# Storing the last staged batch of a sliding-window copy in parts, the rows that may spill first

## The chip, the cores and the metric

The kernel runs on one core of a Trainium2 chip. The metric is the device time of one execution in microseconds (us), lower is better. The program does no arithmetic at all: it only moves data with the core's 16 DMA engines.

## The reference

The input is a float32 array of 32 batches, 4096 rows of 256 values. The output holds 127 windows per batch, each of 64 rows, one starting every 32 rows.

```python
def setup_inputs():
    batch, length, dim = (32, 4096, 256)
    window_size = 64
    stride = 32
    ...

def reference(x, window_size, stride):
    batch, length, dim = x.shape
    n_windows = (length - window_size) // stride + 1
    result = np.zeros((batch, n_windows, window_size, dim), dtype=np.float32)
    for i in range(n_windows):
        start = i * stride
        result[:, i] = x[:, start:start + window_size].copy()
    return result
```

Call 32 rows (32 KB) a block. A batch has 128 blocks, and window w is block w followed by block w + 1. So almost every block is written twice, as half 0 of one window and as half 1 of the one before it.

## The kernel before

Three queues work at once.

- The Sync queue copies windows of the "direct" batches from DRAM to DRAM.
- The Scalar queue serves eleven "staged" batches (1, 4, ... 31). It loads a batch into on-chip memory, one block per partition, and stores it twice, once as all the halves 0 and once as all the halves 1. A store has 128 partitions but a batch has only 127 windows, so a store writes a row or two past its own batch. These spilled rows land in a neighbouring batch's windows, which must be written afterwards.
- The GpSimd queue writes those neighbours' windows, each after the staged stores beside it have landed.

The last staged batch is 31. Its stores spill into windows 125 and 126 of batch 30, and the Sync queue repairs these with one 128 KB copy at the very end.

```python
    def store(self, q, t, b, half, shift):
        w = b * self.nw - half - shift
        return q.dma_start(
            out=self.oap(2 * w + half, [[2 * self.blk, self.nb], [1, self.blk]]),
            in_=t[:, :],
            max_dma_last_dim=OUT,
        )
...
    # class Staging
    def store(self, q, g):
        n, i = divmod(g, len(self.tiles))
        q.wait_ge(self.loaded[i], 16 * (n + 1))
        for half in (0, 1):
            self.c.store(q, self.tiles[i], self.batches[g], half, self.shift(g)).then_inc(self.stored[i], 16)
...
        # GpSimd queue
        count(c.windows(ring_r, last, 112, 4), rest)
        count(c.columns(ring_r, last, 116, 9), rest)
        # Sync queue: the last copy, windows 125 and 126 of batch 30
        st.wait_stored(ring_d, len(staged) - 1)
        count(c.columns(ring_d, last, 125, 2), done)
        for sem in (done, near, rest):
            ring_d.wait_ge(sem, total[sem])
```

Of the kernel before, what the change touches and what calls it, by code (L numbers as in the profile page):

```python
# [11 lines left out]
class Copier:  # L12
# [36 lines left out]
    def load(self, q, t, b, shift):  # L49

        return q.dma_start(
            out=t[:, :],
            in_=self.xap(b * self.nb - shift, [[self.blk, self.nb], [1, self.blk]]),
            max_dma_last_dim=IN,
        )

    def store(self, q, t, b, half, shift):


        w = b * self.nw - half - shift  # L60
        return q.dma_start(
            out=self.oap(2 * w + half, [[2 * self.blk, self.nb], [1, self.blk]]),
            in_=t[:, :],
            max_dma_last_dim=OUT,
        )


class Staging:


    def __init__(self, c, tc, pool, dtype, batches, bufs, shifts):
# [2 lines left out]
        self.loaded = [tc.alloc_semaphore(f"loaded{i}") for i in range(bufs)]  # L74
        self.stored = [tc.alloc_semaphore(f"stored{i}") for i in range(bufs)]

    def shift(self, g):
        return self.shifts.get(self.batches[g], 0)

# [6 lines left out]
    def store(self, q, g):  # L86
        n, i = divmod(g, len(self.tiles))
        q.wait_ge(self.loaded[i], 16 * (n + 1))
        for half in (0, 1):
            self.c.store(q, self.tiles[i], self.batches[g], half, self.shift(g)).then_inc(self.stored[i], 16)  # L90

    def wait_stored(self, q, g):
        n, i = divmod(g, len(self.tiles))
# [12 lines left out]
@with_exitstack  # L106
def kernel(
    ctx: ExitStack,
    tc: tile.TileContext,
    x: bass.AP,  # L110
    window_size: bass.AP,
    stride: bass.AP,
    out: bass.AP,
):
    nc = tc.nc
    W, S = int(window_size), int(stride)
    B, L, D = x.shape
    n_win = (L - W) // S + 1
    assert out.shape == (B, n_win, W, D)
    c = Copier(x, out, B, L, D, W, S, n_win)  # L120
    staged = [*range(1, B, 3)]
    direct = [b for b in range(B) if b not in staged]
    pool = ctx.enter_context(tc.tile_pool(name="xb", bufs=1))



    st = Staging(c, tc, pool, x.dtype, staged, 6, {0: -1, B - 1: 1})
    ring_d, ring_s, ring_r = nc.sync, nc.scalar, nc.gpsimd
    done = tc.alloc_semaphore("done")
    near = tc.alloc_semaphore("near")  # L130
    rest = tc.alloc_semaphore("rest")
    total = {done: 0, near: 0, rest: 0}

    def count(dma, sem):
        dma.then_inc(sem, 16)
        total[sem] += 16

    per, loads, stores = 6, 6 * 17, 34
    todo = 7 * len(direct)
    turns = share = 0  # L140
    with tc.tile_critical():  # L141
        st.run(ring_s)

        for b in direct:
            w = 0 if b - 1 not in staged else 8 if b + 1 in staged and b + 1 < B - 1 else 15
            for j in range(7):
                todo -= 1
                sem = near if todo == 2 else done
                share += 90 if turns % (loads + per * stores) < loads else 12
                if share >= 120:  # L150
                    share -= 120
                    turns += 4
                    count(c.windows(ring_d, b, w, 16, 0), done)
                    count(c.windows(ring_d, b, w, 16, 1), sem)
                else:
                    turns += 3
                    count(c.windows(ring_d, b, w, 16), sem)
                w += 16
                if todo == 7:
                    count(c.windows(ring_d, B - 1, c.nw - 1, 1, 1, 2048), done)  # L160
                    if 0 in staged:
                        count(c.windows(ring_d, 0, 0, 1, 0, 2048), done)

        ring_r.wait_ge(near, 16)
        pieces = (32768,)
        last = B - 2
        for i, b in enumerate(direct[:-1]):
            for g, n in enumerate(staged):
                if abs(n - b) == 1:
                    st.wait_stored(ring_r, g)  # L170
            parts = [(0, 15)] if b - 1 in staged else [(112, 15)]
            if b - 1 in staged and b + 1 in staged:
                parts = [(0, 8), (120, 7)]
            for w, n in parts:
                count(c.windows(ring_r, b, w, n, None, pieces[i % len(pieces)]), rest)


        count(c.windows(ring_r, last, 112, 4), rest)
        count(c.columns(ring_r, last, 116, 9), rest)
        st.wait_stored(ring_d, len(staged) - 1)  # L180
        count(c.columns(ring_d, last, 125, 2), done)
        for sem in (done, near, rest):
            ring_d.wait_ge(sem, total[sem])


# [33 lines left out]
```

## Time and profile before

| | |
|---|---|
| time, three runs | 752.45 us median (752.31 to 753.29) |
| time, five runs | 753.07 us median (752.31 to 753.29) |
| span of the execution in the trace | 743.6 us |
| summed rate over the span | 421 GB/s |

The trace is of an execution that was about 1% quicker than the timed ones.

From the page of the kernel before. The rows are the busy share of the DMA engines and their rate in 40 slices of the span; then the packets; then each queue's packets, MB and share of the 16 engines' time (q1 is the Sync queue, q10 the Scalar queue, q0 the GpSimd queue); then what was read from and written to DRAM.

```profile
span 743.6 us, 309 instructions
DMA  9999999999999999999999999999999999999995
GB/s 369 430 429 433 433 437 428 425 422 434 422 420 419 438 423 414 431 428 423 423 431 413 424 427 436 432 426 428 433 425 433 423 427 432 423 426 436 423 428 241
DMA packets 18098, 313.26 MB, mean 421 GB/s; under 512 B 4144, under 2 KB 4144, under 8 KB 4336
q1 hardware_dynamic: 7952, 154.32, 48.9%
q10 hardware_dynamic: 8976, 138.41, 43.9%
q0 software_dynamic: 1168, 20.51, 6.5%
HBM read 220.95 MB, written 267.09 MB: 656 GB/s over the span
```

The engines never rest until the last slice. The "under 512 B" packets are completion packets of 4 bytes: in this trace the Sync queue's 200 DMAs have 3200 of them and the Scalar queue's 33 have 528, 16 to a DMA, as many as there are engines, and just as many increments of their semaphores are recorded. They took 9 ns in the mean.

The waits of the Sync queue (us in total, times, longest), and the issue of its last copy in the timeline (start, duration), both of the kernel before:

```profile
SPq L44 <- DMA out_dram<-xb: 179.3, 1, 179.3
SPq L141 <- DMA out_dram<-in_x_dram: 1.2, 1, 1.2
SPq L183 <- DMA out_dram<-in_x_dram: 0.6, 1, 0.6
```

```profile
738.18 0.58 SPq L44 DMA_DIRECT2D out_dram<-in_x_dram  x1
```

L44 is the copy: it waits for the stores until 738.18. Then the GpSimd queue's last landing is waited for (L183, 0.6 us, until 739.40), and then the copy's own landing (L141, 1.2 us more). This 1.2 us is what the change can hide.

### The profile page before, as it was taken

The page shows a single profiled execution, that of the slowest core. Times are in us where ns is not written, and L with a number is a line of the kernel's source. Part 1 is how long each engine was busy: PE and PEld are TensorE (multiplying, and loading weights), DVE is VectorE, ACT ScalarE, POOL GpSimd, SP SyncE. Part 2 cuts the span into 40 slices and gives each one's busy share as a digit, 9 for nine tenths or more (in the row PEclk, how much of TensorE's full clock was granted, in tenths as well). Part 3 has the DMA queues.
Part 4 walks back from the last instruction along what each step waited for, and adds up shares of the span by engine and source line. Part 5 has one row for each costly group of instructions (what it writes and reads, how often), then busy time and mean ns, then how long its engine had stood idle before and what let it go on. Part 6 is the DMA issues. An engine that isn't in the chain of part 4 may idle for free.

```text
span 743.6 us, 309 instructions
## 1 busy us (share of the span) xinstructions
POOL 12.8 (2%) x26
## 2 busy tenths in 40 slices
POOL 0000000000000000000000000000000000130100
DMA  9999999999999999999999999999999999999995
GB/s 369 430 429 433 433 437 428 425 422 434 422 420 419 438 423 414 431 428 423 423 431 413 424 427 436 432 426 428 433 425 433 423 427 432 423 426 436 423 428 241
DMA packets 18098, 313.26 MB, mean 421 GB/s; under 512 B 4144, under 2 KB 4144, under 8 KB 4336
## 3 DMA queue, kind: packets, MB, share of 16 engines
q1 hardware_dynamic: 7952, 154.32, 48.9%
q10 hardware_dynamic: 8976, 138.41, 43.9%
q0 software_dynamic: 1168, 20.51, 6.5%
q14 instruction: 2, 0.02, 0.0%
HBM read 220.95 MB, written 267.09 MB: 656 GB/s over the span
## 4 chain that ended last, share of the span: by engine, by line
another core or an unknown queue 92%; POOL 2%; issue 0%; POOLq 0%; SPq 0%
POOL out_dram L34 2%; POOL out_dram L44 0%; POOLq L214 0%; SPq L141 0%; POOLq L94 0%
## 5 line engine op out<-in xcount | busy, mean ns | idle before, releaser
L34 POOL DMA_DIRECT2D out_dram<-in_x_dram x21 | 12.0, 576 | 686.7 <-DMA out_dram<-in_x_dram 647.0
L44 POOL DMA_DIRECT2D out_dram<-in_x_dram x1 | 0.6, 581 | 0.0
L200 POOL MEMSET const-float32-0.0<- 128x1 f32 x1 | 0.1, 99 | 0.2 <-issue 0.2
L200 POOL MEMSET const-bfloat16-1.0<- 128x1 bf16 x1 | 0.1, 102 | 0.0
L200 POOL MEMSET const-float32-1.0<- 128x1 f32 x1 | 0.1, 99 | 0.0
L200 POOL MEMSET const-uint8-127<- 128x1 uint8 x1 | 0.1, 99 | 0.0
## 6 DMA issues: line engine op xcount, KB each, us to landing
out_dram<-in_x_dram SPq DMA_DIRECT2D x96, 1024.0 KB, 100.8
out_dram<-xb ACTq DMA_DIRECT2D x22, 4096.0 KB, 142.5
out_dram<-in_x_dram SPq DMA_DIRECT2D x102, 512.0 KB, 89.1
xb<-in_x_dram ACTq DMA_DIRECT2D x11, 4096.0 KB, 122.0
out_dram<-in_x_dram POOLq DMA_DIRECT2D x20, 960.0 KB, 37.8
out_dram<-in_x_dram POOLq DMA_DIRECT2D x1, 576.0 KB, 40.3
out_dram<-in_x_dram POOLq DMA_DIRECT2D x1, 256.0 KB, 36.8
out_dram<-in_x_dram SPq DMA_DIRECT2D x1, 128.0 KB, 2.5
```

The lines of the kernel that those rows point to most:

```text
L34: return q.dma_start(out=self.oap((b * self.nw + w0) * 2 + h, [[2 * blk, n], row]), in_=self.xap(b * self.nb + w0 + h, [[blk, n], row]), m ...
L44: return q.dma_start(out=self.oap((b * self.nw + w0) * 2, [[part, 16], [2 * self.blk, n], row]), in_=self.xap(b * self.nb + w0, [[part, 16 ...
L200: nc = _bacc.Bacc("TRN2", target_bir_lowering=False, num_devices=1)
```

## The change

The intent is to issue the last copy before the stores are finished. The rows that may spill are partitions 0 and 1 of half 1 and partition 0 of half 0. So half 1 goes out first, then partitions 0 to 31 of half 0, and only these count for the copy's wait. The other 96 partitions follow on a semaphore of their own. That four of the parts take 16 partitions each, 4 apart, was my guess at a quicker shape; no record of the kernel before showed it.

```diff
-    def store(self, q, t, b, half, shift):
-        w = b * self.nw - half - shift
+    def store(self, q, t, b, half, shift, p0=0, n=128, step=1):
+        w = b * self.nw - half - shift + p0
         return q.dma_start(
-            out=self.oap(2 * w + half, [[2 * self.blk, self.nb], [1, self.blk]]),
-            in_=t[:, :],
+            out=self.oap(2 * w + half, [[2 * step * self.blk, n], [1, self.blk]]),
+            in_=t[p0 : p0 + (n - 1) * step + 1 : step, :],
             max_dma_last_dim=OUT,
         )
 ...
+        self.ended = tc.alloc_semaphore("ended")
 ...
-        for half in (0, 1):
-            self.c.store(q, self.tiles[i], self.batches[g], half, self.shift(g)).then_inc(self.stored[i], 16)
+        parts = [(0, 0, 128, 1), (1, 0, 128, 1)]
+        if g == len(self.batches) - 1:
+            parts = [(1, 0, 128, 1), (0, 0, 32, 1)]
+            rest = [(0, 96, 32, 1)] + [(0, 32 + k, 16, 4) for k in range(4)]
+        for half, *p in parts:
+            self.c.store(q, self.tiles[i], self.batches[g], half, self.shift(g), *p).then_inc(self.stored[i], 16)
+        if g == len(self.batches) - 1:
+            for half, *p in rest:
+                self.c.store(q, self.tiles[i], self.batches[g], half, self.shift(g), *p).then_inc(self.ended, 16)
+            self.ended_total = 16 * len(rest)
 ...
-        for sem in (done, near, rest):
-            ring_d.wait_ge(sem, total[sem])
+        total[st.ended] = st.ended_total
+        for sem, n in total.items():
+            ring_d.wait_ge(sem, n)
```

## The prediction

The sum of the prediction came to 752.45 - 0.95 + 0.35 = 751.85 us. The +0.35 us was my estimate, of 0.2 to 1 us, for longer packets of the partial stores, and what it rested on was not shown.

> **What bounds the kernel now.** It only moves data. The page's slice row shows the 16 DMA engines at 9 tenths in 39 of 40 slices, about 425 GB/s; the packet records give 27 GB/s per engine, one packet open on each (16 KB out of SBUF 0.61 us, 32 KB DRAM to DRAM 1.21 us). The change removes no bytes, so only the last slice (5 tenths, 241 GB/s) can gain.
>
> **The tail before**, from semaphore landings and packets, in us of the 743.6 us span:
> - One engine runs 2 us behind the other 15 (the second store of the last staged batch lands on 15 engines by 736.07, on the last at 738.16). The others have no data packets from 736.8; the late one works until 738.94.
> - The Sync queue waits for both whole stores of that batch, because a few rows spill into batch 30's windows 125 and 126. It issues the 128 KB copy of these windows at 738.18; first packets 739.55, landing 740.65.
> - The GpSimd queue's last copy lands at 739.38 on the late engine, whatever happens to the stores. The last wait ends at 740.67; some 3 us of closing barriers follow.
>
> So only 740.65 - 739.38 = 1.27 us of the copy is exposed.
>
> **What the change does.** The rows that can spill (half 1, then partitions 0 to 31 of half 0) are stored first and counted alone. Per engine 12 of 32 packets follow them, about three quarters of the 22.5 us of one whole store, so the copy should be issued at about 721 and land by 726, hidden. Its packets remain: two of 0.16 us per engine, 0.32 us, now before the end on the late engine. Gain: 1.27 - 0.32 = 0.95 us. Added: five DMAs on the Scalar queue (five 9 ns completion packets per engine; issue about 0.5 us each when unblocked, over 100 us ahead of need) and one wait of 0.03 us.
>
> [...] No record of this kernel shows a partial store. In the tail stores get about 188 GB/s (GpSimd's copies the other 240)[...].
>
> **Time.** 752.45 - 0.95 + 0.35 = 751.85; I say 751.8 us, range 750.9 to 752.8. Faster by over 2%: 0.01; within: 0.98; slower: 0.01.
>
> **What would show it.** Right: the copy is issued near 721; the final wait ends near 739.7 to 740.2, released by the late engine's GpSimd or store landing; the summed rate stays near 430 GB/s, with store packets over 0.61 us only between about 717 and 728. Wrong: the copy is still issued after 735, or its landing ends the span, or partial stores' packets take 1.2 us.
>
> **What would make it wrong.** [...] parts that use fewer than 16 engines; the late engine lagging more, or not at all (then the gain could reach 2 us); noise: the three runs before span 1 us, as much as the effect.

## The result

The changed kernel took 752.92 us (median of five, 751.71 to 753.81) against 753.07 us before (752.31 to 753.29). The ratio is 1.0001, 95% interval 0.9988 to 1.0015: the same time. In a second set of five, on another occasion, it was 1.0000 (0.9987 to 1.0012). A ratio is the mean time of one kernel's fast runs over that of the other's of the same rounds, so it is not quite the ratio of the medians. The prediction, 751.8 us with a range to 752.8, missed.

The same lines of the page of the changed kernel:

```profile
span 752.0 us, 315 instructions
GB/s 370 425 424 419 431 425 430 425 422 420 420 411 420 429 419 418 422 410 427 418 416 410 419 422 430 430 427 431 431 423 418 421 421 431 417 416 427 422 413 251
DMA packets 18178, 313.26 MB, mean 417 GB/s; under 512 B 4224, under 2 KB 4224, under 8 KB 4416
q10 hardware_dynamic: 9056, 138.41, 44.0%
HBM read 220.95 MB, written 267.09 MB: 649 GB/s over the span
```

Only q10 has more packets, 9056 - 8976 = 80. These are five more DMAs with 16 completion packets each. The waits of the Sync queue and the copy in the timeline, of the changed kernel:

```profile
SPq L44 <- DMA out_dram<-xb: 168.0, 1, 168.0
SPq L195 <- DMA out_dram<-in_x_dram: 15.5, 1, 15.5
```

```profile
732.53 0.58 SPq L44 DMA_DIRECT2D out_dram<-in_x_dram  x1
```

So the early copy works as meant. It is issued at 732.53 and has landed by 741.34, and the Sync queue then waits 15.5 us for the GpSimd queue's last copy. The wait for the copy's landing has gone from the end. Yet the time did not change.

**How the end was compared.** For each trace I took the moment at which 20 MB were still to be moved, and cut the time from there to the end of the span into four terms:

- *mean finish*: the mean time per engine that is filled with data packets (checked again from the packet records: their times after that moment, summed and divided by 16, agree within 0.1 us), leaving out the late copy where the copy comes after everything else. Small packets and gaps are not in it; they fall into the next term;
- *late engine*: how long after that the last engine finishes;
- *landing*: from the last of these data packets to the last landing of any DMA;
- *closing*: the barriers after the last landing.

| trace | mean finish | late engine | landing | closing | sum |
|---|---|---|---|---|---|
| before | 46.13 | 3.06 | 1.71 | 2.99 | 53.89 |
| before, r1 | 46.85 | 1.62 | 1.65 | 3.00 | 53.12 |
| before, r7 | 46.99 | 1.65 | 1.62 | 3.00 | 53.25 |
| change | 47.48 | 3.08 | 0.42 | 3.43 | 54.40 |
| change, r2 | 47.85 | 3.22 | 0.46 | 3.42 | 54.95 |
| change, r8 | 47.54 | 2.32 | 0.43 | 3.43 | 53.72 |

Landing fell by 1.22 us in the mean, close to the 1.27 us that the prediction read from the trace. Closing rose by 0.43 us and mean finish by 0.97 us (46.66 to 47.62), and these two took it back. The late engine scatters by 1.5 us between traces of one and the same kernel. The mean finish of before leans on its first trace, the quicker execution. Between traces of the same occasion mean finish rose by 1.00 us (r1 to r2) and by 0.55 us (r7 to r8).

### The profile page after: what moved, and what is told of

The parts are those of the page before. It is cut to its first block, busy times and chain, and to the rows that moved or that the text cites. A ratio compares the mean times of both kernels' runs of the same rounds, so it can differ in the third digit from the quotient of the medians.

```text
span 752.0 us, 315 instructions
## 1 busy us (share of the span) xinstructions
POOL 12.8 (2%) x26
## 3 DMA queue, kind: packets, MB, share of 16 engines
q1 hardware_dynamic: 7952, 154.32, 48.7%
q10 hardware_dynamic: 9056, 138.41, 44.0%
q0 software_dynamic: 1168, 20.51, 6.6%
HBM read 220.95 MB, written 267.09 MB: 649 GB/s over the span
## 4 chain that ended last, share of the span: by engine, by line
another core or an unknown queue 92%; POOL 2%; issue 0%; POOLq 0%; SPq 0%
POOL out_dram L34 2%; POOL out_dram L44 0%; POOLq L226 0%; SPq L152 0%; POOLq L105 0%
```

## The experiments

The expectations name these theories. Theory a: stores of parts with 32 partitions in a row are slow, which loses what the early copy gains, and parts with partition step 4 are not (the reason that I supposed is not shown by any run). Theory b: the gain is there and the scatter of the bulk hides it. Theory c: the order of the last waits costs 0.43 us. Theory d: the parts hurt by where their rows lie in DRAM. Theory e: parts cost nothing in the bulk. Theory f came last: every packet of a queue, however small, uses up the queue's turn on its engine. "Shape theories" are a and d, which blame the parts' partitions or rows.

### Replicas, and the two halves of the change (r1 to r4)

r1 is the kernel before and r2 the changed kernel, unaltered. r3 keeps the parts and gives up the early copy; r4 keeps the early copy and uses parts that all have partition step 4.

```diff
 r3, from the change
         st.wait_stored(ring_d, len(staged) - 1)
+        ring_d.wait_ge(st.ended, st.ended_total)
         count(c.columns(ring_d, last, 125, 2), done)
 r4, from the change
-            parts = [(1, 0, 128, 1), (0, 0, 32, 1)]
-            rest = [(0, 96, 32, 1)] + [(0, 32 + k, 16, 4) for k in range(4)]
+            parts = [(1, 0, 128, 1), (0, 0, 32, 4)]
+            rest = [(0, k, 32, 4) for k in range(1, 4)]
```

> The kernel before, run against itself, for the noise and for a second trace of its tail. Both theories [...] expect a ratio of 1.000 with an interval of about 0.15% either way. In its trace the copy of windows 125 and 126 should be issued within 1 us of the last landing of the stores and land 2.3 to 2.7 us later, the stores' packets of the last 40 us should take 0.61 to 0.62 us in the mean, and the data packets of 15 engines should end within 3 us of each other.

> The changed kernel again, for a second trace and ten timed runs in all. Theory a [...]: the stores' packets of the last 40 us again take about 3% over 0.611 us in the mean, the summed rate falls to about 400 GB/s between the first partial store and the four parts, and the engines' last data packets spread over about 5 us where before they spread over 2 us beside the late engine. Theory b (noise only): packets at 0.611 us, spread as before, and the last landing 1 us nearer to the end of the bulk. Ratio 0.999 to 1.001 in both.

> The stores in parts as in the change, but the Sync queue waits for all parts before it issues the copy, so the splitting is there and the early copy is not. Against the kernel before it shows the cost of the parts alone: theory a expects 1 to 2.5 us more (ratio 1.0015 to 1.003), theory b expects the same time (below 1.0005). In its trace the copy should be issued right after the last part lands and the span should end about 3 us plus 2.5 us after that.

> The early copy kept, but half 0 of the last batch goes out as four parts of 32 partitions with partition step 4 (0, 4, ... 124 first, it holds the spilling row)[...]. Theory a expects the tail's store packets back at 0.61 to 0.62 us, the copy still issued about 15 us before the end, and the gain of about 1 us to appear (ratio 0.998 to 1.000). Theory b expects what the changed kernel shows.

The kernel before ran at 755.33 us here.

| run | median us | ratio to before (95%) | mean finish | late engine | landing | closing | sum |
|---|---|---|---|---|---|---|---|
| r1, before | 755.18 | 0.9990 (0.9977 to 1.0003) | 46.85 | 1.62 | 1.65 | 3.00 | 53.12 |
| r2, change | 755.67 | 1.0000 (0.9987 to 1.0012) | 47.85 | 3.22 | 0.46 | 3.42 | 54.95 |
| r3, parts only | 755.70 | 1.0008 (0.9995 to 1.0021) | 47.10 | 2.41 | 2.56 | 2.99 | 55.05 |
| r4, step 4 | 754.72 | 0.9996 (0.9979 to 1.0013) | 47.43 | 2.49 | 0.42 | 3.42 | 53.77 |

The time alone cannot settle half a microsecond: the interval is about 1 us either way, and even before against itself comes out at 0.9990. The traces say more. (A figure "from 8 to 3 MB left" and the like is my own sum over the trace's packet records in the stretch in which that much was still to be moved.) The parts raise the mean finish even without the early copy (r3), and parts with step 4 raise it too (r4). Against theory a, the DRAM copies' packets in the tail were as much too long as the stores' (in r2 from 8 to 3 MB left, 4.7% over 1.213 us and 4.7% over 0.611 us; in r1 2.0% and 1.7%), although neither end of a DRAM copy is in the on-chip memory.

### The closing (r5, r6), and two more traces (r7, r8)

```diff
 r5, from the change; r6, from r4
-        for sem, n in total.items():
-            ring_d.wait_ge(sem, n)
+        for sem in (rest, done, near, st.ended):
+            ring_d.wait_ge(sem, total[sem])
```

In the built program the first of these waits stands last, in the branch itself (in the trace of before, the first of its three, for the copy's landing, is the branch at 740.67 us).

> The changed kernel with its four last waits in another order: the semaphore of the GpSimd queue's copies, which lands last, now stands in the wait of the branch itself, and the three that landed long before come first. From the traces so far the closing (last landing to the end of the span) is 2.99 to 3.00 us where the last wait of all is the one that is released last (before, and the late copy) and 3.42 to 3.43 us where it is the first of four (the changed kernel, step 4). Theory c (the order of the waits costs 0.43 us): closing back at 3.0 us. Rival (the closing grows with the fourth semaphore or with the longer program): it stays at 3.4 us. The time itself should move by 0.4 us, within the noise: ratio 0.998 to 1.001.

> Parts with partition step 4 and the waits in the other order[...]. Then closing 3.0 us, last landing 0.45 us behind the last data packet, and the time from 20 MB left to the end of the span about 53.3 us or less (before: 53.9 and 53.1; the change: 54.4 and 55.0); ratio 0.997 to 0.9995. If instead the wait was never worth 1 us because the engines end 2 to 3 us apart whatever is done, the sum stays at 53 to 54 us and the ratio at 0.999 to 1.001.

> A third trace of the kernel before. Sum from 20 MB left to the end 53 to 54.5 us: mean finish of the engines 46 to 47, the late engine 1.5 to 3 us behind, last landing 1.65 to 1.75 us later, closing 3.0 us.

> A third trace of the changed kernel. Theory a [...]: mean finish 47.3 to 48 us after 20 MB are left, about 1 us more than before, of which 0.3 us is the copy's own packets; late engine 2.5 to 3.5 us behind; last landing 0.42 to 0.46 us later; closing 3.4 us; sum 54 to 55 us. Theory b (noise): mean finish as before plus 0.3 us, sum about 53 us.

r5 had a ratio of 1.0010 (0.9997 to 1.0024), r6 of 1.0009 (0.9995 to 1.0022). r7 and r8 are single looks (753.88 and 754.74 us, state unknown). From 20 MB left, r5 summed to 52.90 us, less than any trace of before, and r6 to 53.70 us. Closing was 3.30 us in r5 and r6, so the order is worth 0.13 of the 0.43 us and theory c holds only for that part. The other 0.3 us is one step: from the branch with the last wait to the Sync queue's next signal took 0.14 us in r1 (750.62 to 750.76) and 0.45 us in r2, r5 and r6 (in r5, 748.83 to 749.28). It was short wherever the copy was issued at the very end and its own landing was the last to be waited for. What makes it short I did not find.

In the timed runs the early copy with better waits was no faster than before, as the rival in r6's expectation said. r8 had the mean finish that theory a expected, but its late engine (2.32 us) and its sum (53.72 us) lay below what that theory expected. By now there were seven traces of kernels with parts, all with a mean finish of 47.1 to 47.9 us, whatever their partitions.

### The parts made large (r9 to r12)

If 4 MB of parts cost half a microsecond, 88 MB should cost ten. Here all 22 store halves of the eleven staged batches go out in parts, and the last copy still waits for everything.

```diff
 r9, r10, r11, from before (the store takes p0, n, step as in the change)
+PARTS = [(p, 32, 1) for p in (0, 32, 64, 96)]                                # r9
+PARTS = [(0, 32, 1), (96, 32, 1)] + [(32 + k, 16, 4) for k in range(4)]      # r10
+PARTS = [(k, 32, 4) for k in range(4)]                                       # r11
         for half in (0, 1):
-            self.c.store(q, self.tiles[i], self.batches[g], half, self.shift(g)).then_inc(self.stored[i], 16)
+            for p in PARTS:
+                self.c.store(q, self.tiles[i], self.batches[g], half, self.shift(g), *p).then_inc(self.stored[i], 16)
 r12, from before: all 128 partitions, half a row at a time
+            for c0 in (0, self.c.blk // 2):
+                self.c.store(q, self.tiles[i], self.batches[g], half, self.shift(g), c0, self.c.blk // 2
+                ).then_inc(self.stored[i], 16)
```

> The suspected cost made large: all 22 store halves of the staged batches go out as four parts of 32 consecutive partitions (88 MB in all, where the change has 2 MB of such parts), the last copy still waits for all of them. Theory a [...]: the tail's 0.5 us for 2 MB of such parts becomes about 20 us, ratio 1.02 to 1.04, with store packets several per cent longer and DRAM copies unchanged. Rival d (the parts hurt because of where their rows lie in DRAM, which the packets of DRAM copies in the same stretch, 4 to 7% longer too, point to): DRAM copies grow as much as stores; size unknown. Rival e (partial stores cost nothing in the bulk, only the last few us are uneven): ratio 1.000 to 1.003.

> All 22 store halves as two parts of 32 consecutive partitions and the change's four parts of 16 with partition step 4: half of the bytes in the first kind and half in the second. Theory a: only the 44 MB of the first kind cost, about half of what four parts of 32 cost (ratio 1.01 to 1.02). Rival d: the parts with step 4 (rows 256 KB apart) cost too, so as much as or more than four parts of 32. Rival e: 1.000 to 1.003.

> All 22 store halves as four parts of 32 partitions with step 4[...]. Theory a: no cost, 1.000 to 1.003. Rival d: a cost like that seen in the tail of the step 4 kernel, where the stretch from 8 to 3 MB left took 12.05 us against 11.5 to 11.8 before: 3 to 4%, ratio 1.01 to 1.03. Rival e: 1.000 to 1.003.

> Control for the number of DMAs: all 22 store halves as two DMAs of all 128 partitions and half a row each, packets of 16 KB as before[...]. All theories of the parts' shape expect no cost, ratio 0.998 to 1.002; a cost here would be that of more DMAs or of the order of the packets.

The kernel before ran at 754.91 us. The last two columns say where the loss lies: before or within the last 20 MB, against the mean of r1 and r7, traced on other occasions (699.7 us to that point, 53.2 us after it).

| run | store DMAs | median us | ratio (95%) | lost before | lost after |
|---|---|---|---|---|---|
| r9, 4 x 32 in a row | 88 | 784.97 | 1.0379 (1.0344 to 1.0414) | 12.8 | 20.1 |
| r10, the change's kinds | 132 | 797.16 | 1.0554 (1.0516 to 1.0592) | 22.7 | 19.9 |
| r11, 4 x 32, step 4 | 88 | 766.11 | 1.0151 (1.0130 to 1.0173) | 9.0 | 2.4 |
| r12, half rows | 44 | 761.33 | 1.0082 (1.0062 to 1.0102) | 4.4 | 3.0 |

No theory passed all four. Theory a met r9, but r11's parts all have step 4 and cost 1.5%, and r10, with half its bytes in parts with step 4, costs more than r9. Theory d met r10 and r11, but r12 has the rows, partitions and packet sizes of the kernel before and still costs 0.8%. Theory e is far off. The part of the loss in the bulk grows with the number of DMAs (44, 88, 88, 132). What a DMA adds is its completion packets (352 small packets for the 22 DMAs added in r12). So I looked at how the two busy queues share the engines, in a window of 130 us in which the Scalar queue stores and the Sync queue copies. DMA queues in the window 150 to 280 us, columns packets, MB and share of the engines' time: r1 (before), r12, r11 and, from the next group, r13.

```profile
q1 hardware_dynamic: 1488, 31.46, 57.9%
q10 hardware_dynamic: 1486, 23.04, 42.8%
```

```profile
q1 hardware_dynamic: 1503, 31.79, 59.5%
q10 hardware_dynamic: 1506, 21.92, 41.0%
```

```profile
q1 hardware_dynamic: 1556, 32.90, 62.1%
q10 hardware_dynamic: 1551, 20.30, 38.4%
```

```profile
q1 hardware_dynamic: 1615, 34.21, 67.1%
q10 hardware_dynamic: 1620, 17.73, 33.4%
```

In each of the four the two queues move the same number of packets, to within 0.4%. The engines take turns, one packet from each: in the same window of the first trace of before, 2983 of the 3011 packets begin 3 to 4 ns before another one ends, and if each of them is put after such a one, at least 2949 of these successions change the queue. The counts are equal only with the completions in them: in r1 960 of q1's packets and 1406 of q10's carry data. What I had missed is that a completion packet of 4 bytes and 9 ns counts as a turn. When a store's completion comes up, the other queue gets its next 32 KB packet of 1.21 us, and the stores have moved nothing in return. More DMAs on the store queue mean fewer stores and more DRAM copies.

Why does that lengthen the whole? A DRAM copy reads and writes DRAM, a store only writes it: on the page of before, q1's 154.32, q0's 20.51 and the loads' 46.14 MB add up to the 220.95 MB read, and q1's, q0's and the stores' 92.27 MB to the 267.09 MB written. From the lines above, twice q1's MB plus q10's MB over 130 us is 661 GB/s in r1, 658 in r12, 662 in r11 and 663 in r13. The DRAM traffic stays at 660 GB/s while the mixture changes, so more copies in it mean fewer bytes moved: (31.46 + 23.04) MB in r1, (34.21 + 17.73) MB in r13. The packets show where the time goes: in this window a DRAM copy's took 1.249 us in the mean in r1 and 1.332 us in r13, a store's 0.633 and 0.637 us. The stores left behind then run alone at the end, where the 16 engines move 430 GB/s (r11, 720 to 736 us) and the DRAM traffic is no more than that. That DRAM traffic is the limit is inferred from its constancy in seven kernels; no run lifted it by itself, the quicker first trace of before had 672 GB/s in this window, and a stretch of its tail reached 688 GB/s (from 8 to 5.5 MB left).

The shape of the parts probably matters in a case that the change hardly meets: when stores run alone. DMA packets and queues while only stores run: r9 (parts of 32 in a row) from 728 to 748 us, then r11 (step 4) from 720 to 736 us.

```profile
DMA packets 450, 5.90 MB, mean 295 GB/s; under 512 B 90, under 2 KB 90, under 8 KB 90
q10 hardware_dynamic: 450, 5.90, 100.3%
```

```profile
DMA packets 536, 6.88 MB, mean 430 GB/s; under 512 B 116, under 2 KB 116, under 8 KB 116
q10 hardware_dynamic: 522, 6.88, 100.6%
```

All engines are busy in both, but at 295 against 430 GB/s, and r9 lost 20.1 us in its last 20 MB where r11 lost 2.4. The two runs differ in which partitions a part takes and in where its rows lie in DRAM; which of the two makes the difference, and how, is not shown.

### Turns taken away and given (r13 to r16)

```diff
 r13, from before: stores whole, three DMAs of 16 rows x 4 bytes after each of them
             self.c.store(q, self.tiles[i], self.batches[g], half, self.shift(g)).then_inc(self.stored[i], 16)
+            for _ in range(3):
+                q.dma_start(out=self.scratch[:, k : k + 1], in_=self.c.xap(0, [[self.c.blk, 16], [1, 1]])
+                ).then_inc(self.tiny, 16)          # k counts up: a column of its own each time
 r14 and r16, from the change: one added DMA, and the waits as in r5
-            parts = [(1, 0, 128, 1), (0, 0, 32, 1)]
-            rest = [(0, 96, 32, 1)] + [(0, 32 + k, 16, 4) for k in range(4)]
+            parts = [(1, 0, 128, 1), (0, 0, 64, 2)]
+            rest = [(0, 1, 64, 2)]
 r15, from before: all store halves in two parts
+PARTS = [(k, 64, 2) for k in range(2)]
```

> The kernel before with all its stores whole; after each of the 22 store halves the Scalar queue issues three DMAs of 16 rows of 4 bytes into a scratch tile, which move nothing to speak of but add three small data packets and three completion packets per engine each time (66 of each in all). Theory f (every packet of the store queue, however small, uses up its turn, so the DRAM copies of the Sync queue run ahead and the stores are left over): slower by at least what the step 4 parts everywhere cost (1.015), 1.015 to 1.05; the store queue's share of the bytes in the store stretches falls, and a stretch with stores alone appears near the end. Shape theories [...]: 0.999 to 1.003.

> Early copy with one added DMA only: half 1 whole, then half 0 as two parts of 64 partitions with step 2, and the waits in the better order. Theory f: in the stretch from 5.5 to 3 MB left the stores keep about 180 GB/s of 420 or more (change: 140 to 151 of 398 to 411), mean finish about 47 us after 20 MB are left (before 46.1 to 47.0, change 47.5 to 47.9), last landing 0.4 us after the last data, closing 3.3 us, sum 52 to 53 us; ratio 0.998 to 0.9998. Shape theory: as the changed kernel, sum 53.7 to 55 us, ratio 1.000.

> All 22 store halves as two parts of 64 partitions with step 2. Theory f: it has the 44 store DMAs of the control with half rows (1.0082), so the same cost, 1.006 to 1.010[...]. Shape theories: a cost between none (1.000 to 1.003) and that of the step 4 parts (1.015).

> The same kernel as r14 once more, for a second trace of its tail: sum from 20 MB left to the end 52 to 53.3 us under theory f, 53.7 to 55 us under the shape theory.

The kernel before ran at 754.62 us.

| run | median us | ratio (95%) |
|---|---|---|
| r13, 66 DMAs that move next to nothing | 775.50 | 1.0280 (1.0263 to 1.0297) |
| r15, two parts with step 2 everywhere | 759.71 | 1.0065 (1.0051 to 1.0078) |
| r14, one added DMA | 754.31 | 0.9991 (0.9978 to 1.0004) |
| r16, the same, one look | 753.56 | state unknown |

r13 is the decisive run. No store is touched, no partition or row differs, the added bytes are nothing, and it loses 21 us. Its small packets took 0.010 us in the mean in the window, so they did not hold the engines up themselves. As expected, a stretch with stores alone appears: from 706 to 722 us no other queue moves data. r15 has the 44 DMAs of r12, another shape, and nearly the same cost. Completion packets in the window 150 to 280 us, per engine, against the stores' rate there:

| | r1 | r15 | r12 | r9 | r11 | r10 | r13 (with its tiny data packets) |
|---|---|---|---|---|---|---|---|
| small packets of the store queue per engine | 5.0 | 10.4 | 10.5 | 19.3 | 19.5 | 26.6 | 33.6 |
| stores, GB/s | 177 | 171 | 169 | 156 | 156 | 146 | 136 |
| both queues, GB/s | 419 | 416 | 413 | 407 | 409 | 405 | 400 |

In this mixture the parts' partitions (r9 against r11, both 156 GB/s) make no difference to the stores' rate: it follows the number of small packets.

The same is to be seen in the tail, though less clearly. DMA packets and queues from 733 to 741 us, about 10 to 18 us before the last landing: r1 (before), r2 (change) and r14 (one added DMA).

```profile
DMA packets 184, 3.36 MB, mean 420 GB/s; under 512 B 35, under 2 KB 35, under 8 KB 35
q0 software_dynamic: 91, 1.84, 54.9%
q10 hardware_dynamic: 93, 1.52, 45.5%
```

```profile
DMA packets 204, 3.21 MB, mean 401 GB/s; under 512 B 65, under 2 KB 65, under 8 KB 72
q0 software_dynamic: 100, 2.03, 62.5%
q10 hardware_dynamic: 97, 1.15, 36.0%
```

```profile
DMA packets 196, 3.38 MB, mean 422 GB/s; under 512 B 51, under 2 KB 51, under 8 KB 51
q0 software_dynamic: 98, 2.00, 59.7%
q10 hardware_dynamic: 98, 1.38, 41.1%
```

Again the numbers of packets are nearly equal. In r1 all of q10's 93 packets carry 16 KB (1.52 MB). In r2 the 1.15 MB are 70 such packets, so 27 of 97 turns went to small ones; the stores move a quarter less, and the sum falls from 420 to 401 GB/s. In r14 14 of 98 turns are small, and the sum is back at 422 GB/s. The other traces scatter around this: 434 GB/s in r7 (before), 412 in r8 (change), 426 in r18 (one added DMA).

| added store DMAs, traces | mean finish | less 0.32 us where the copy lies within it |
|---|---|---|
| 0 (before, r1, r7) | 46.13, 46.85, 46.99 | the same |
| 1 (r14, r16, r18) | 46.70, 47.06, 46.99 | 46.38, 46.74, 46.67 |
| 3 (r4, r6) | 47.43, 47.49 | 47.11, 47.17 |
| 5 (change, r2, r8, r5) | 47.48, 47.85, 47.54, 47.50 | 47.16, 47.53, 47.22, 47.18 |
| 5, late copy (r3) | 47.10 | the same |

The last batch's two whole halves become three, five or seven DMAs. There is a step from one to three added DMAs, and between three and five there is none to speak of. The parts' shape changes along with their number here, and the first trace of before is the quicker one, so this table alone does not show the cause. r14's sum, 53.17 us, was just above the 52 to 53 us expected.

### The balance restored in the change, and the best version again (r17, r18)

r17 keeps the change's parts and gives the GpSimd queue empty turns as well. r18 is r14 with five more rounds.

```diff
 r17, from the change, in the loop of the GpSimd queue's copies
                 count(c.windows(ring_r, b, w, n, None, pieces[i % len(pieces)]), rest)
+            if i in (14, 15, 16):
+                ring_r.dma_start(out=st.scratch[:, k : k + 1], in_=c.xap(0, [[c.blk, 16], [1, 1]])
+                ).then_inc(st.tiny, 16)
```

> The changed kernel with three DMAs of 16 rows of 4 bytes added to the GpSimd queue, after its 15th, 16th and 17th copies, which fall into the stretch of the parts (about 730 to 737 us): six empty turns per engine for that queue, against the five that the parts add to the store queue. Theory f: the stores' rate in the stretch from 5.5 to 3 MB left goes back from 140 to 151 GB/s to 165 GB/s or more, and the sum there from 400 to 407 to 412 or more; mean finish 47.0 to 47.3 us after 20 MB left instead of 47.5 to 47.9; ratio 0.998 to 1.001. Shape theory: the sum stays at 398 to 411 GB/s and the mean finish at 47.5 us or more.

> One added DMA and the waits in the better order, five rounds more. The three traces before of the unchanged kernel sum to 53.1 to 53.9 us from 20 MB left, the two of this version to 52.9 and 53.2: a gain of about 0.4 us, ratio 0.9995, expected between 0.998 and 1.0005; not to be told from 1 unless the gain is larger than the traces say.

The kernel before ran at 755.11 us. r17 took 755.30 us, ratio 1.0004 (0.9981 to 1.0028). r18 took 754.48 us, ratio 0.9991 (0.9972 to 1.0010).

r17 moved the shares, and missed the main number, the stores' rate. Its empty turns came earlier than I had placed them: the added DMAs landed from 720.9 to 735.3 us, two thirds of the landings by 729. From 11 to 8 MB left the stores rose to 215 GB/s and from 8 to 5.5 MB to 205 (change: 161 to 167 and 159 to 162), so turns do set the shares in the tail too. But from 5.5 to 3 MB left they were still at 142 GB/s, where 165 or more was expected (the sum there was 416, as expected), and the sum was 402 GB/s in the first of these stretches. There 7 of the stores' 98 packets took 1.2 to 1.6 us instead of 0.61, and DRAM traffic was only 588 GB/s, below the 660 of the bulk; what held the sum down there is not shown. Mean finish was 47.14 us, as expected, the late engine was 3.66 us behind, and closing was 3.68 us with its five waits. The sum, 54.90 us, was as high as the change's, so giving turns back in this way saved nothing.

r14 and r18 gave 0.9991 twice, and their traces with r16 sum to 53.17, 52.91 and 53.98 us from 20 MB left, against 53.42 us in the mean before. That is the best version tried, and it is not told apart from the kernel before.

## Why the prediction was wrong, point by point

- **What bounds the kernel: half right.** The engines are busy throughout. But I read 27 GB/s per engine as the limit; in the bulk the rate falls below the 430 GB/s at which the engines move r11's stores alone (419 GB/s in r1, 400 in r13) when DRAM copies gain in the mixture, at a constant 660 GB/s of DRAM traffic.
- **"So only 740.65 - 739.38 = 1.27 us of the copy is exposed": right.** Landing fell by 1.22 us.
- **"Its packets remain ... 0.32 us": not contradicted.** No run isolates it.
- **The copy "issued at about 721 and land by 726": right in kind, late.** It was issued at 732.53, 736.38 and 734.92 us (the change's trace, r2, r8), 14.2 to 15.7 us before the last data packet instead of about 18, since the stores had lost share. It stayed hidden all the same.
- **"Added: five DMAs on the Scalar queue (five 9 ns completion packets per engine ...)": the first of two steps that failed.** I priced a completion packet at its 9 ns, 0.045 us for five. It costs a turn; the stores lose share and the data packets get longer. Mean finish rose by 0.97 us, of which 0.32 us at most is the copy; the other 0.65 us goes with the parts. Its size is uncertain: between traces of the same occasion the rise less 0.32 us is 0.68 us (r1 to r2) and 0.23 us (r7 to r8). That a turn costs time is shown in the bulk, by r13. That turns are the whole of this rise in the tail is inferred; r17, which should have settled it, missed the stores' rate that it forecast.
- **"And one wait of 0.03 us": the second step that failed.** Closing rose by 0.43 us: 0.13 us from the order of the waits (r5), 0.3 us in the step after the branch, cause open.
- **The 0.35 us in "752.45 - 0.95 + 0.35", for the shape of the parts: about half of the loss, on the wrong bill.** In the mixture the parts' partitions made no difference to the stores' rate (156 GB/s in r9 and in r11). A loss that goes with partitions in a row, or with their rows in DRAM, shows when stores run alone (295 against 430 GB/s). That my 0.35 us, an estimate whose grounds are not shown, covered about half of the 0.65 us was luck.
- **The sum.** Predicted: -1.27 (landing) + 0.32 + 0.35 (copy and parts, both in mean finish) = -0.60 us. Measured: -1.22 (landing) + 0.97 (mean finish) + 0.43 (closing) = +0.18 us. Of the 0.78 us between them, closing is 0.43, mean finish 0.30 and landing 0.05 us. The late engine adds 0.76 us in the means of three traces each, but scatters between 1.62 and 3.06 us in the kernel before alone; whether parts make it later stays open. The timed ratio, whose interval reaches from 0.9 us below to 1.1 us above, agrees with a loss of 0.18 us and cannot show it.
- **Noise.** The median of before itself moved from 752.45 to 753.07 us with two more runs, more than the distance by which the time missed the range.

## What to carry to other kernels

A DMA's completion packet may cost nothing in bytes and still cost its queue a turn on every engine (here 66 added DMAs of 64 bytes slowed a kernel of 754.6 us by 2.8%); where two busy queues take turns packet by packet, count each queue's packets, small ones too, before you split one of its DMAs. To wake a dependent early, split off as few DMAs as will do (here one) and let the semaphore that lands last be the one that is waited for last (worth 0.13 us here). Even so, the best version here could not be told from the kernel before. A gain of 1 us in 750 must be read from the tails of several traces, term by term, because the timed runs cannot show it.
